# One layer's expert sum: rows of V gathered for one token block, float32 V products for the other

## The chip, the cores and the metric

The kernel runs on one core of a Trainium2 chip. The metric is the device time of one execution in microseconds (us). The engines are TensorE (PE; its weight loads are shown as PEld), VectorE (DVE), ScalarE (ACT), GpSimd (POOL) and SyncE (SP), which here only issues transfers. Sixteen DMA engines move the data of all queues.

## The reference

A network of two layers, followed by a second network, on 256 latent and 256 context tokens of 1024 channels. The part that matters is the expert layer (PEER) at the end of layer 1, on the 256 latent tokens:

```python
def peer_ffn(h, w_query, sub_keys, expert_u, expert_v):
    ...
    idx = jnp.take_along_axis(cand_i, pos, axis=-1).reshape(t_count, PEER_HEADS * PEER_TOPK)
    gate = jax.nn.softmax(top_s, axis=-1).reshape(t_count, PEER_HEADS * PEER_TOPK).astype(h.dtype)
    ...
    def block(args):
        tb, ib, gb = args
        act = jax.nn.gelu(jnp.einsum('pkd,pd->pk', expert_u[ib], tb), approximate=False) * gb
        return jnp.einsum('pk,pkd->pd', act, expert_v[ib])
```

`idx` holds the best 16 of 128 x 128 experts for each token and each of 8 heads; a `block` is 128 tokens. So each token has 128 chosen experts out of 16384. For each of them the token's vector is multiplied with a row of U (`peer_u`), passed through Gelu, weighted by its gate, and the rows of V (`peer_v`) are summed with these weights. U and V have 16384 rows of 1024 float32 numbers each, 64 MiB a table.

## The kernel before

The program is written with tiles and pools; the order of instructions on each engine and all waits come from a scheduler, which can move an instruction ahead of its place in the program when its inputs and buffers are free. Where the text calls `self.follow(d, mark[0])`, DVE instruction `d` is kept behind the one in `mark`. SP's queue, ScalarE's queue and GpSimd's queue each issue their transfers in order; an issue that waits for its buffer holds those behind it.

The function `peer1` does the expert layer of layer 1. Its 256 tokens are two blocks of 128, and each block takes another way.

- **The gathering block** (j=0) fetches, for each of its 128 slots (one slot is one chosen expert of every token), the 128 rows of U that its tokens chose, with an indirect DMA on GpSimd's queue (128 rows of 4 KB, 512 KB), into one of NR=6 buffers `rows`. One DVE instruction (L1281) multiplies them with the tokens `hn` and adds up along the row into a column of `dots`. `tick(n)` issues n such pairs from the list `todo`.
- **The dense block** (j=1) multiplies its tokens `hd` with all of U, in float32: `mm1` (L1253 to L1270) takes four row blocks of `peer_ut` (the transposed U) through four buffers `uf` (L1261, 512 KB each on SP's queue) and does 32 matmuls of 128 columns, then Gelu into `act`, [expert in block, block, token]. There are 32 calls.

The stages follow each other like this. First the queries, keys and the search for the best 16 (L1381 to L1394), with a `mm1` call and some gathers of U between. Then the one-hot stage of the dense block (L1461 to L1468), here called **B**: to put the gates in the layout of `act`, 32 steps of four tokens each build one-hot matrices, `oneR` (L1433) and three of four `oneL` (L1444) on DVE, the fourth on ScalarE, multiply them on PE (L1445) and copy them into `stage` (L1446); after every fourth step GpSimd multiplies `act` with the finished gates (L1466) or copies the gates in ahead of it (L1468). `between` runs after each step: it spreads the waiting U gathers over 27 steps and calls `mm1` after every third.

Then **C** (L1470 to L1480): Gelu on `dots`, times the gates, transposed, and a second one-hot stage of 32 steps for the gathering block, whose results go to a DRAM array `gd` (L1479); the remaining `mm1` calls stand between. At its end the pools of B and C are closed.

Then **D** (L1487 to L1499), the loop over 128 blocks of 128 rows of V, for both token blocks together: a block of V is loaded (`wf`, 512 KB on SP's queue) and split into a high and a low float32r part, 512 columns at a time, by ScalarE and DVE (`wsl`, `split`, L215 and L216); so are the activations (`gd` reloaded as `gt`, and `act`); and `mm3` (L249 to L251) does three float32r matmuls for each of two token blocks and two halves of the columns, twelve of 512 columns in all, into four PSUM accumulators. After the loop `_peer_out` transposes each sum and adds it into the residual `xT`.

The function `peer` of layer 0 is not touched, but is looked at: it also loads V blocks, loads `peer_ut` and gathers rows, of U and then of V, for one of its token blocks (L1154 to L1170), where the V rows are summed on DVE by L1169.

Of the kernel before, what the change touches and what calls it, by code (L numbers as in the profile page):

```python
# [170 lines left out]
class Net:  # L171
# [1031 lines left out]
    def peer1(self, xT, a, sh, gcol):  # L1203
# [3 lines left out]

# [6 lines left out]
        dr = pool("q_dr", bufs=1, space=DRAM)  # L1214
# [8 lines left out]
        def pf():  # L1223
            return fp.tile([128, 4, 128], F32, name="pf", bufs=6)
# [6 lines left out]
        hn = f0.tile([128, 8, 128], F32, name="hn")  # L1231
# [12 lines left out]
        gidx = f0.tile([128, 128], I32, name="gidx")  # L1244
        dots = f0.tile([128, 128], F32, name="dots")
# [28 lines left out]

        def tick(n):
            for _ in range(min(n, len(todo))):
                j = todo.pop(0)
                ug = f0.tile([128, 1024], F32, name="rows", bufs=NR)
                nc.gpsimd.indirect_dma_start(out=ug, out_offset=None, in_=A["peer_u1"],
                                             in_offset=bass.IndirectOffsetOnAxis(ap=gidx[:, j:j + 1], axis=0))  # L1280
                d = nc.vector.scalar_tensor_tensor(ug, ug, 1.0, hnf, op0=ALU.mult, op1=ALU.mult,  # L1281
                                                   accum_out=dots[:, j:j + 1])
                if mark[0] is not None:
                    self.follow(d, mark[0])
# [122 lines left out]
        gd = dr.tile([8, 128, 128, 16], F32, name="gd")  # L1407
        cols = []
        for j in (1, 0):
            ii = fs.tile([128, 128], I32, name="ii")  # L1410
            i2 = fl(idx[:, j])
            nc.vector.tensor_copy(ii, i2)
            nc.vector.tensor_single_scalar(ii, ii, 7, op=ALU.arith_shift_right)
            i1 = fs.tile([128, 128], F32, name="i1")
            nc.vector.tensor_copy(i1, ii)
            nc.vector.scalar_tensor_tensor(i2, i1, -128.0, i2, op0=ALU.mult, op1=ALU.add)
            p = pf()
            for c, t in enumerate((i1, i2, fl(gate[:, j]))):
                nc.tensor.transpose(p[:, c], t, self.ident)
            T = fs.tile([128, 5, 128], F32, name="igT", bufs=2)  # L1420
            nc.scalar.copy(T[:, 0], p[:, 0])
            nc.scalar.copy(T[:, 2:4], p[:, 1:3])
            mark[0] = nc.vector.tensor_scalar_mul(T[:, 1:5:3], T[:, 2:4], -1.0)
            cols.append(T)

        def onehot(T, t0, sg, engs, after):
# [28 lines left out]
        def between(q):  # L1455
            step[0] += 1
            tick(-(-len(todo) // max(1, 28 - step[0])))
            if step[0] % 3 == 0:
                mm1()

        for n in range(8):  # L1461
            sg = stage()
            onehot(cols[0], 16 * n, sg, "avvv", between)
            o, nb = 16 * n, 4 * done[0]
            gated[0] = o + 16
            nc.gpsimd.tensor_mul(act[:, 0:nb, o:o + 16], act[:, 0:nb, o:o + 16], sg[:, 0:nb])  # L1466
            if nb < 128:
                nc.gpsimd.tensor_copy(act[:, nb:128, o:o + 16], sg[:, nb:128])  # L1468

        T = cols[1]  # L1470
        nc.scalar.activation(dots, dots, AF.Gelu)
        nc.vector.tensor_mul(dots, dots, fl(gate[:, 0]))
        p = pf()
        nc.tensor.transpose(p[:, 0], dots, self.ident)
        nc.vector.tensor_copy(T[:, 3], p[:, 0])
        for g in range(8):
            sg = stage()
            onehot(T, g * 16, sg, "pvvv", lambda q: mm1() if q % 2 else None)
            nc.sync.dma_start(gd[g], sg)  # L1479
        assert done[0] == 32  # L1480
# [4 lines left out]
        acc = {(j, h): pacc.tile([128, 512], F32, name=f"acc{j}{h}") for j in range(2) for h in range(2)}  # L1485
        gt = None
        for b in range(128):  # L1487
            if b % 8 == 0:
                gt = ds_.tile([128, 8, 8, 16], F32, name="gt", bufs=2)
                nc.scalar.dma_start(gt, gd[:, :, b:b + 8, :].rearrange("g p i t -> p g i t"))  # L1490
            ah = ds_.tile([128, 256], F32R, name="ah", bufs=3)
            al = ds_.tile([128, 256], F32R, name="al", bufs=3)
            s3 = lambda t: t[:, 0:128].rearrange("p (g t) -> p g t", t=16)
            self.split(s3(ah), s3(al), gt[:, :, b % 8])
            self.split(ah[:, 128:], al[:, 128:], act[:, b])
            for h, w in enumerate(self.wsl(A["peer_v1"][b * 128:(b + 1) * 128], 512)):
                for j in range(2):
                    s = slice(j * 128, (j + 1) * 128)
                    self.mm3(acc[j, h], (ah[:, s], al[:, s]), w, b == 0, b == 127)  # L1499
        for j in range(2):  # L1500
            o = ds_.tile([128, 2, 512], F32, name="of", bufs=2)
            for h in range(2):
                nc.scalar.copy(o[:, h], acc[j, h])
            self._peer_out(2 + j, o, xT, gcol, pmm)
# [644 lines left out]
```

## Time and profile before

| | us |
|---|---|
| median of 3 runs | 3469.16 (3463.92 to 3498.61) |
| profiled execution | 3467.91 |
| its span, first to last instruction | 3466.1 |
| stage B, 2419.7 to 2537 | 117.3 |
| stage C, 2537 to 2626 | 89.0 |
| stage D, 2626 to 2978 | 352.0 |
| mean granted PE clock | 0.958 of full |

The stage borders are times from the span's start, read off the first and last instructions of the lines named above. The busy time of an engine is the union of its instructions, so that pipelined matmuls are not counted twice; a float32 matmul leaves two records. "DMA share" is the mean busy share of the 16 DMA engines (it can pass 1 a little), and GB/s what they moved.

### The profile page before, as it was taken

Reading aid. Unit: us, or ns where it says so; the run is one execution under the profiler, and the core shown is the slowest. Engines: PE = TensorE matmul, PEld = TensorE weight load, DVE = VectorE, ACT = ScalarE, POOL = GpSimd, SP = SyncE. Lnnn points to the kernel's source line nnn. Section 1 sums busy time; section 2 is a strip of 40 time slices with the busy share of each in tenths; the row PEclk is TensorE's granted clock in tenths of the full one; section 3 lists DMA queues with packets and bytes.
Section 4 is the critical chain, followed back from the end, with each engine's and each line's share of the span. In section 5 each row is a group of like instructions: output and inputs, shape, how many; then the busy total and the mean of one; then the engine's idle time right before and its main releaser. Section 6 shows DMA issues by size and latency. Waiting matters only on the chain. (4 is left out here: it accounts for less than half of the span.)

```text
span 3466.1 us, 54363 instructions
## 1 busy us (share of the span) xinstructions
PE 3164.8 (91%) x19470; PEld 2676.5 (77%) x19470; DVE 2438.0 (70%) x5726; ACT 1586.1 (46%) x3325; POOL 865.6 (25%) x781
## 2 busy tenths in 40 slices
PE   7989998898899999999999899965798999889899
PEld 4655657788889999999988658864787888777898
DVE  4664575688868777878877674787856666676666
ACT  3333334545963334433334463111535666653655
POOL 0010010466943333344432001444632000000000
PEclk9999999899999999999999999987899999899999
DMA  6355243233479898898877215998766777443465
GB/s 234 110 154 163 92 153 106 71 104 111 194 262 332 305 322 310 304 328 305 306 265 239 85 38 202 374 371 339 254 207 201 217 217 217 135 119 115 131 187 172
DMA packets 263855, 723.62 MB, mean 209 GB/s; under 512 B 22816, under 2 KB 97440, under 8 KB 259488
## 3 DMA queue, kind: packets, MB, share of 16 engines
q1 hardware_dynamic: 178496, 492.58, 42.6%
q0 software_dynamic: 55296, 201.35, 17.0%
q10 hardware_dynamic: 29792, 26.22, 2.3%
q8 instruction: 153, 2.51, 0.3%
q14 instruction: 118, 0.97, 0.1%
HBM read 681.00 MB, written 38.80 MB: 208 GB/s over the span
## 5 line engine op out<-in xcount | busy, mean ns | idle before, releaser
L215 ACT CAST wh<-wf 128x512 fp32r<-128x512 f32 (+1 forms) x906 | 560.3, 619 | 756.3 <-PE mm L250 288.3
L216 DVE TENSOR_TENSOR wl<-wf,wh 128x512 fp32r<-128x512 f32 (+1 forms) x820 | 563.7, 689 | 275.8 <-ACT wh L215 272.3
L251 PE MATMUL mm<-h_hi,wl 128*128 128x384 f32 x1024 | 347.2, 339 | 7.2 <-POOL wl L216 5.5
L249 PE MATMUL mm<-h_hi,wh 128*128 128x384 f32 x1024 | 348.8, 341 | 1.1 <-ACT wh L215 1.0
L250 PE MATMUL mm<-h_lo,wh 128*128 128x384 f32 x1024 | 346.0, 338 | 0.0
L251 PE MATMUL acc<-vh,al 128*128 128x512 f32 x768 | 300.7, 392 | 0.0
L250 PE MATMUL acc<-vl,ah 128*128 128x512 f32 x768 | 300.5, 391 | 0.0
L249 PE MATMUL acc<-vh,ah 128*128 128x512 f32 x768 | 298.7, 389 | 0.0
L1263 PE MATMUL mm<-hd,uf 128*128 128x128 f32 x2048 | 258.9, 285 | 28.8 <-DMA uf<-in_peer_ut_dram 24.5
L1263 PEld LDWEIGHTS mm<-hd,uf 128*128 128x128 f32 x2048 | 249.2, 201 | 34.1 <-DMA uf<-in_peer_ut_dram 14.8
L1157 POOL DMA_INDIRECT rows<-in_peer_v_dram,gidx x128 | 162.4, 1269 | 293.9 <-DVE hn L1169 273.5
L215 ACT CAST vh<-vf 128x512 fp32r<-128x512 f32 x256 | 158.8, 620 | 157.8 <-PE acc L251 151.4
L216 DVE TENSOR_TENSOR vl<-vf,vh 128x512 fp32r<-128x512 f32 x256 | 176.9, 691 | 67.0 <-ACT vh L215 65.1
L1157 POOL DMA_INDIRECT rows<-in_peer_u_dram,gidx x128 | 146.4, 1144 | 307.0 <-DVE rows L1163 297.9
L216 POOL TENSOR_TENSOR wl<-wf,wh 128x512 fp32r<-128x512 f32 x86 | 115.3, 1348 | 421.7 <-PE pa L581 251.5
L249 PE MATMUL acc<-wh,ah 128*128 128x512 f32 x512 | 200.6, 392 | 7.8 <-ACT ah L215 6.7
L1281 DVE SCALAR_TENSOR_TENSOR rows<-rows,hn 128x1024 f32<-128x1024 f32 x128 | 165.9, 1307 | 57.1 <-DMA rows<-in_peer_u_dram,gidx 56.8
L251 PEld LDWEIGHTS mm<-h_hi,wl 128*128 128x128 f32 x1024 | 193.5, 189 | 8.8 <-POOL wl L216 6.8
L251 PE MATMUL acc<-wh,al 128*128 128x512 f32 x512 | 200.2, 391 | 0.0
L250 PE MATMUL acc<-wl,ah 128*128 128x512 f32 x512 | 200.1, 391 | 0.0
L249 PEld LDWEIGHTS mm<-h_hi,wh 128*128 128x128 f32 x1024 | 193.9, 189 | 5.4 <-ACT wh L215 1.7
L250 PEld LDWEIGHTS mm<-h_lo,wh 128*128 128x128 f32 x1024 | 193.9, 189 | 3.7
(698 smaller groups left out, 7604.1 us busy)
## 6 DMA issues: line engine op xcount, KB each, us to landing
vf<-in_peer_v_dram SPq DMA_DIRECT2D x128, 512.0 KB, 5.9
wf<-in_peer_ut_dram SPq DMA_DIRECT2D x128, 512.0 KB, 6.3
uf<-in_peer_ut_dram SPq DMA_DIRECT2D x128, 512.0 KB, 6.7
wf<-in_peer_v_dram SPq DMA_DIRECT2D x128, 512.0 KB, 3.9
wa<-in_ada_w_dram SPq DMA_DIRECT2D x96, 512.0 KB, 4.3
gd<-stage SPq DMA_DIRECT2D x32, 1024.0 KB, 3.9
gt<-gd SPq DMA_DIRECT2D x48, 512.0 KB, 7.7
wf<-in_ffn_up_dram SPq DMA_DIRECT2D x44, 512.0 KB, 3.6
```

Of the source, the lines that this page charges most:

```text
L215: nc.scalar.copy(hi, src)
L216: return (eng or nc.vector).tensor_sub(lo, src, hi.bitcast(F32))
L249: nc.tensor.matmul(out, l[0], r[0], start=start, stop=False)
L250: nc.tensor.matmul(out, l[0], r[1], start=False, stop=False)
L251: nc.tensor.matmul(out, l[1], r[0], start=False, stop=stop)
L1157: nc.gpsimd.indirect_dma_start(out=t, out_offset=None, in_=A[src], in_offset=bass.IndirectOffsetOnAxis(ap=gidx[:, j:j + 1], axis=0))
L1263: nc.tensor.matmul(p[:, i], wf[:, k * 128:(k + 1) * 128], hd[:, k], start=(k == 0), stop=(k == 7))
L1281: d = nc.vector.scalar_tensor_tensor(ug, ug, 1.0, hnf, op0=ALU.mult, op1=ALU.mult, accum_out=dots[:, j:j + 1])
```

## The change

The gathering block now gathers rows of V as it gathered rows of U, and DVE adds them up; the one-hot stage C, `gd` and the gathering block's part of the loop over V go. The dense block's products with V become plain float32 matmuls without the split, two a block instead of twelve.

- `rows(src, j)` issues one gather of `peer_u1` or `peer_v1` into one of the six buffers, `tick_v(n)` issues n gathers of V from the list `left`, each with a DVE instruction that adds row times `dots` column to the accumulator `gf`. `rows`, `hn`, `gidx` and `dots` move to the pool that lives through the whole function; `gacc` takes the buffer of `hn`.
- `between` has done all U gathers after step 16, then weights `dots`, clears `gacc` on GpSimd, and does one V gather a step in the steps 17 to 32. `mm1` is called after every fourth step.
- The loop over V calls `mm1` in every fifth round until all 32 calls are out, loads a block of V into one of six buffers `vf`, does two float32 matmuls of 512 columns, and spreads the remaining 112 V gathers over its rounds.

```diff
         hf = fs.tile([128, 8, 256], F32, name="hf")
         self.norm_split(xT, [(256, 256, 0, a, sh)], None, None, lambda: pf().rearrange("p a b -> p (a b)"), t2, keep=hf)
-        hn = f0.tile([128, 8, 128], F32, name="hn")
+        hn = sb.tile([128, 8, 128], F32, name="hn")
...
         tv = f0.tile([128, nt, 8, 16], F32, name="tv")
         idx = f0.tile([128, nt, 8, 16], F32, name="idx")
         gate = f0.tile([128, nt, 8, 16], F32, name="gate")
-        gidx = f0.tile([128, 128], I32, name="gidx")
-        dots = f0.tile([128, 128], F32, name="dots")
+        gidx = sb.tile([128, 128], I32, name="gidx")
+        dots = sb.tile([128, 128], F32, name="dots")
...
         todo = []
+        def rows(src, j):
+
+            t = sb.tile([128, 1024], F32, name="rows", bufs=NR)
+            nc.gpsimd.indirect_dma_start(out=t, out_offset=None, in_=A[src],
+                                         in_offset=bass.IndirectOffsetOnAxis(ap=gidx[:, j:j + 1], axis=0))
+            return t
+
         def tick(n):
             for _ in range(min(n, len(todo))):
                 j = todo.pop(0)
-                ug = f0.tile([128, 1024], F32, name="rows", bufs=NR)
-                nc.gpsimd.indirect_dma_start(out=ug, out_offset=None, in_=A["peer_u1"],
-                                             in_offset=bass.IndirectOffsetOnAxis(ap=gidx[:, j:j + 1], axis=0))
+                ug = rows("peer_u1", j)
                 d = nc.vector.scalar_tensor_tensor(ug, ug, 1.0, hnf, op0=ALU.mult, op1=ALU.mult,
                                                    accum_out=dots[:, j:j + 1])
+                if mark[0] is not None:
+                    self.follow(d, mark[0])
+
+        left = list(range(128))
+
+        def tick_v(n):
+            for _ in range(min(n, len(left))):
+                j = left.pop(0)
+                d = nc.vector.scalar_tensor_tensor(gf, rows("peer_v1", j), dots[:, j:j + 1], gf,
+                                                   op0=ALU.mult, op1=ALU.add)
                 if mark[0] is not None:
                     self.follow(d, mark[0])
         nc.vector.tensor_mul(gate, gate, sm[:, :, :, None].to_broadcast(s4))
...
-        gd = dr.tile([8, 128, 128, 16], F32, name="gd")
-        cols = []
-        for j in (1, 0):
...
-        def onehot(T, t0, sg, engs, after):
+        ii = fs.tile([128, 128], I32, name="ii")
+        i2 = fl(idx[:, 1])
+        nc.vector.tensor_copy(ii, i2)
+        nc.vector.tensor_single_scalar(ii, ii, 7, op=ALU.arith_shift_right)
+        i1 = fs.tile([128, 128], F32, name="i1")
+        nc.vector.tensor_copy(i1, ii)
+        nc.vector.scalar_tensor_tensor(i2, i1, -128.0, i2, op0=ALU.mult, op1=ALU.add)
+        p = pf()
+        for c, t in enumerate((i1, i2, fl(gate[:, 1]))):
+            nc.tensor.transpose(p[:, c], t, self.ident)
+        T = fs.tile([128, 5, 128], F32, name="igT")
+        nc.scalar.copy(T[:, 0], p[:, 0])
+        nc.scalar.copy(T[:, 2:4], p[:, 1:3])
+        mark[0] = nc.vector.tensor_scalar_mul(T[:, 1:5:3], T[:, 2:4], -1.0)
+
+        def onehot(t0, sg, engs, after):
...
         step = [0]
         def between(q):
+            nonlocal gf, gacc
             step[0] += 1
-            tick(-(-len(todo) // max(1, 28 - step[0])))
-            if step[0] % 3 == 0:
+            if step[0] <= 16:
+                tick(-(-len(todo) // (17 - step[0])))
+            if step[0] == 16:
+                nc.scalar.activation(dots, dots, AF.Gelu)
+                nc.vector.tensor_mul(dots, dots, fl(gate[:, 0]))
+                gacc = sb.tile([128, 8, 128], F32, name="hn").rearrange("p (h a) b -> p h (a b)", h=2)
+                gf = gacc.rearrange("p h d -> p (h d)")
+                nc.gpsimd.memset(gacc, 0.0)
+            if step[0] > 16:
+                tick_v(1)
+            if step[0] % 4 == 0:
                 mm1()
+        gf = gacc = None
         for n in range(8):
             sg = stage()
-            onehot(cols[0], 16 * n, sg, "avvv", between)
+            onehot(16 * n, sg, "avvv", between)
             o, nb = 16 * n, 4 * done[0]
             gated[0] = o + 16
             nc.gpsimd.tensor_mul(act[:, 0:nb, o:o + 16], act[:, 0:nb, o:o + 16], sg[:, 0:nb])
             if nb < 128:
                 nc.gpsimd.tensor_copy(act[:, nb:128, o:o + 16], sg[:, nb:128])
-
-        T = cols[1]
-        nc.scalar.activation(dots, dots, AF.Gelu)
-        nc.vector.tensor_mul(dots, dots, fl(gate[:, 0]))
-        p = pf()
-        nc.tensor.transpose(p[:, 0], dots, self.ident)
-        nc.vector.tensor_copy(T[:, 3], p[:, 0])
-        for g in range(8):
-            sg = stage()
-            onehot(T, g * 16, sg, "pvvv", lambda q: mm1() if q % 2 else None)
-            nc.sync.dma_start(gd[g], sg)
-        assert done[0] == 32
         fr.close()
         ds_ = pool("q_ds", bufs=1)
         pacc = pool("q_acc", bufs=1, space=PSUM)
-        acc = {(j, h): pacc.tile([128, 512], F32, name=f"acc{j}{h}") for j in range(2) for h in range(2)}
-        gt = None
+        acc = [pacc.tile([128, 512], F32, name=f"acc{h}") for h in range(2)]
+        mark[0] = None
         for b in range(128):
-            if b % 8 == 0:
-                gt = ds_.tile([128, 8, 8, 16], F32, name="gt", bufs=2)
-                nc.scalar.dma_start(gt, gd[:, :, b:b + 8, :].rearrange("g p i t -> p g i t"))
-            ah = ds_.tile([128, 256], F32R, name="ah", bufs=3)
-            al = ds_.tile([128, 256], F32R, name="al", bufs=3)
-            s3 = lambda t: t[:, 0:128].rearrange("p (g t) -> p g t", t=16)
-            self.split(s3(ah), s3(al), gt[:, :, b % 8])
-            self.split(ah[:, 128:], al[:, 128:], act[:, b])
-            for h, w in enumerate(self.wsl(A["peer_v1"][b * 128:(b + 1) * 128], 512)):
-                for j in range(2):
-                    s = slice(j * 128, (j + 1) * 128)
-                    self.mm3(acc[j, h], (ah[:, s], al[:, s]), w, b == 0, b == 127)
-        for j in range(2):
-            o = ds_.tile([128, 2, 512], F32, name="of", bufs=2)
+            if b % 5 == 0:
+                mm1()
+            v = ds_.tile([128, 1024], F32, name="vf", bufs=6)
+            nc.sync.dma_start(v, A["peer_v1"][b * 128:(b + 1) * 128])
             for h in range(2):
-                nc.scalar.copy(o[:, h], acc[j, h])
-            self._peer_out(2 + j, o, xT, gcol, pmm)
+                nc.tensor.matmul(acc[h], act[:, b], v[:, h * 512:(h + 1) * 512], start=(b == 0), stop=(b == 127))
+            tick_v(-(-len(left) // max(1, 126 - b)))
+        assert done[0] == 32 and not left and not todo
+        o = ds_.tile([128, 2, 512], F32, name="of")
+        for h in range(2):
+            nc.scalar.copy(o[:, h], acc[h])
+        self._peer_out(3, o, xT, gcol, pmm)
+        self._peer_out(2, gacc, xT, gcol, pmm)
...
```

## Rows read from the trace of the kernel before

**Rows 1.** The page: span; busy time of each engine.

```profile
span 3466.1 us, 54363 instructions
...
PE 3164.8 (91%) x19470; PEld 2676.5 (77%) x19470; DVE 2438.0 (70%) x5726; ACT 1586.1 (46%) x3325; POOL 865.6 (25%) x781
```

**Rows 2.** Windows B, C, D: busy us (instructions) by engine, clock, DMA share, GB/s.

```profile
2419.70:2537.00 117.30, 89.02 (x618) 83.46 (x617) 106.70 (x213) 60.58 (x116) 67.40 (x45) 0.82 0.68 228
2537.00:2626.00 89.00, 80.45 (x672) 76.69 (x672) 47.05 (x129) 35.52 (x39) 42.52 (x32) 1.00 0.64 231
2626.00:2978.00 352.00, 347.94 (x1523) 287.87 (x1524) 237.28 (x509) 209.38 (x510) 0.00 (x0) 0.99 0.70 211
```

**Rows 3.** PE groups in B+C; `mm1` in C; one call.

```profile
L1263 PE MATMUL mm<-hd,uf 128*128 128x128 f32 x768 | 98.4, 283 | 0.9 <-ACT act L1270 0.6 <-DMA uf<-in_peer_ut_dram 0.4
L1445 PE MATMUL pf<-oneR,oneL 128*128 128x128 f32 x512 | 82.9, 306 | 32.2 <-DVE oneR L1433 12.1 <-DVE oneL L1444 9.3 <-POOL oneL L1444 7.3
...
2537.00:2626.00 89.00, 48.09 (x418) 47.31 (x418) 1.00 0.64 231
...
2562.90 7.31 PE L1263 MATMUL mm<-hd,uf 128*128 128x128 f32 x64
```

**Rows 4.** DVE's timeline, one step of B: start, duration, instruction.

```profile
2424.05 0.68 DVE L1433 TENSOR_TENSOR oneR<-io,igT 128x512 f32<-128x512 f32 x1
...
2425.43 1.21 DVE L1281 SCALAR_TENSOR_TENSOR rows<-rows,hn 128x1024 f32<-128x1024 f32 x1
...
2426.57 1.21 DVE L1281 SCALAR_TENSOR_TENSOR rows<-rows,hn 128x1024 f32<-128x1024 f32 x1
...
2427.72 0.68 DVE L1433 TENSOR_TENSOR oneR<-io,igT 128x512 f32<-128x512 f32 x1
```

**Rows 5.** U gathers and U products from B on.

```profile
L1279 POOL DMA_INDIRECT rows<-in_peer_u_dram,gidx x28: 933/1056/2132, 2419.5 to 2499.8; - x28
...
DMA to landing us min/median/max: 4.2/5.7/8.2
...
L1281 DVE SCALAR_TENSOR_TENSOR rows<-rows,hn 128x1024 f32<-128x1024 f32 x32 | 38.5, 1215 | 0.0
```

**Rows 6.** Layer 0: V product; last U product and the memset.

```profile
L1169 DVE SCALAR_TENSOR_TENSOR hn<-rows,dots,hn x128: 1277/1279/1287, 1460.5 to 1919.5; 128x1024 f32<-128x1024 f32 x128
...
1455.65 1.22 DVE L1163 SCALAR_TENSOR_TENSOR rows<-rows,hn 128x1024 f32<-128x1024 f32 x1
...
1456.94 0.95 POOL L1190 MEMSET hn<- 128x1024 f32 x1 [0.40 <-DVE rows L1163]
```

**Rows 7.** Float32 matmuls of 512 columns, elsewhere in the kernel.

```profile
2057.95 3.60 PE L1605 MATMUL psc<-kT,qz 128*128 128x512 f32 x8
...
L1605 PE MATMUL psc<-kT,qz x64: 590/592/697, 2018.6 to 2075.8; 128*128 128x512 f32 x64
```

**Rows 8.** Windows and DMA of 2340 to 2360.

```profile
2340.00:2360.00 20.00, 16.04 (x123) 14.96 (x122) 11.80 (x31) 2.09 (x6) 8.17 (x9) 0.95 1.03 418
...
q0 software_dynamic: 1164, 4.24, 51.9%
q1 hardware_dynamic: 1129, 4.10, 50.3%
...
uf<-in_peer_ut_dram SPq DMA_DIRECT2D x8, 512.0 KB, 8.4
rows<-in_peer_u_dram,gidx POOLq DMA_INDIRECT x8, 14.4
```

**Rows 9.** Window in layer 0.

```profile
1250.00:1750.00 500.00, 500.00 (x2529) 455.11 (x2528) 397.10 (x580) 198.55 (x362) 190.65 (x155) 1.00 0.90 311
```

**Rows 10.** Two windows ahead of B; SP's queue in the first.

```profile
2300.00:2320.00 20.00, 5.19 (x22) 4.24 (x21) 19.71 (x47) 1.78 (x5) 12.00 (x10) 0.70 0.95 349
2370.00:2420.00 50.00, 18.34 (x127) 17.18 (x126) 35.55 (x85) 5.09 (x14) 28.06 (x25) 0.66 0.79 293
...
q1 hardware_dynamic: 505, 1.88, 25.5%
```

More of the change, by code (lines that the diff above doesn't have):

```diff
@@ L1213, in peer1 @@
         pmm = pool("q_mm", bufs=1, space=PSUM)
-        dr = pool("q_dr", bufs=1, space=DRAM)
         hd = sb.tile([128, 8, 128], F32, name="hd")
@@ L1406, in peer1 @@
         fl = lambda t: t.rearrange("p a b -> p (a b)")
-        gd = dr.tile([8, 128, 128, 16], F32, name="gd")
-        cols = []
-        for j in (1, 0):
[L1410 to L1416, printed above, removed]
-            p = pf()
[L1418 to L1424, printed above, removed]
-        def onehot(T, t0, sg, engs, after):
+        ii = fs.tile([128, 128], I32, name="ii")
[13 more added lines that the diff above has]
+        def onehot(t0, sg, engs, after):
             for q in range(4):
@@ L1468, in peer1 @@
                 nc.gpsimd.tensor_copy(act[:, nb:128, o:o + 16], sg[:, nb:128])
-        T = cols[1]
-        nc.scalar.activation(dots, dots, AF.Gelu)
-        nc.vector.tensor_mul(dots, dots, fl(gate[:, 0]))
-        p = pf()
-        nc.tensor.transpose(p[:, 0], dots, self.ident)
-        nc.vector.tensor_copy(T[:, 3], p[:, 0])
-        for g in range(8):
-            sg = stage()
-            onehot(T, g * 16, sg, "pvvv", lambda q: mm1() if q % 2 else None)
-            nc.sync.dma_start(gd[g], sg)
-        assert done[0] == 32
         fr.close()
```

## Prediction

> **What bounds the kernel now.** I read the page's header and its table of engines first [rows 1]: TensorE (PE) is busy 91% of a 3466.1 us span, but that is an average over stages. The change touches only `peer1`, so the next view is the table of windows over the part of `peer1` that it rewrites [rows 2]. Three stages follow each other there: B, the one-hot stage of the dense token block (117.3 us); C, the one-hot stage of the gathering block (89.0 us); D, the loop over 128 row blocks of V (352.0 us); 558.3 us together. The reader should see that each has another limit. In B VectorE (DVE) is busy 106.7 of 117.3 us. In C PE is busy 80.5 of 89. In D PE is busy 347.9 of 352 at nearly full clock, 352/128 = 2.75 us for the twelve matmuls of a block, while DMA moves only 211 GB/s. Before B, the queries already stream `peer_ut` and gather rows of U side by side; the change leaves that alone, and it is the nearest picture of what D turns into.
>
> **Stage C goes.** The second `onehot` loop, the transposes for j=0, the eight stores of `gd` and their reload fall away: 89.0 us. Not all of it is saved: of the twelve first products (`mm1`) still open at the start of B (768 records, 64 to a call), 418 records, 6.5 calls, ran in C [rows 3]. They move into B or D and are counted there, each with its four loads on SP's queue, its Gelu on ScalarE and its multiplication on DVE.
>
> **Stage B gets longer.** DVE sets B: PE's waits for its one-hots end on DVE first of all [rows 3]. One step there is one `oneR` and three `oneL`; in the timeline two gather products and one such step take 2427.72-2424.05 = 3.67 us, of it 1.145 us for each product and 1.38 us for the rest [rows 4]. The 32 U products left at the start of B [rows 5] come two a step in 16 steps instead of two and later one, which changes nothing in sum. New are 16 V products, one a step in the second half. None runs here before, but layer 0 has the same instruction at 1.279 us [rows 6]: 16 x 1.28 = 20.5 us, all on the bounding engine. At the change from U to V the accumulator takes the buffer of `hn`: GpSimd's memset waits for the last U product, the first V product for the memset and its gather, and the next one-hots stand behind that product on DVE. Layer 0 makes the same turn: the memset starts at 1456.94, 0.07 us after the end of the last U product, and takes 0.95 us [rows 6]. The turn costs between nothing and 8 us (a gather of 1.06 us to issue and 5.7 to land in B [rows 5], behind the memset); I take 2, nearest to layer 0's turn. Gelu on `dots` waits on ScalarE for the same product, with copies of `stage` behind it, inside that time. GpSimd has room: 67.4 us busy of 117.3, plus 16 gathers of 1.1 us. One `mm1` in four steps instead of three gains nothing, since PE isn't what B waits for. B: 117.3+20.5+2 = 140 us, with bounds of 127 (the new work first fills DVE's 10.6 us of idle time) and 146.
>
> **Stage D, TensorE.** Per block, twelve float32r matmuls become two float32 matmuls of 512 columns. A float32 matmul leaves two records; eight records of that shape in a row take 3.60 us, the last of them 0.59, so starts are (3.60-0.59)/7 = 0.43 us apart [rows 7]. A matmul is 0.86 us, a block 1.72 instead of 2.75, 128 blocks 220 us. Weight loads are in that figure. The splits on ScalarE and DVE vanish, but PE hardly waited for them; they save nothing. Nine `mm1` calls are written into the loop, but calls move ahead of their place: 20 of 32 were done when B began, though the program had put out 15. I count five of the twelve in D, bounds 3 and 9. A call is 7.3 us [rows 3], so PE has 220+37 = 257 us of work. PE no longer sets the loop.
>
> **Stage D, transfers.** Now 112 gathers of V rows run beside 128 V loads and 20 `uf` loads, 524288 bytes each: 260 x 0.524 = 136.3 MB. The row that prices this is the stretch from 2340 to 2360, where `uf` loads and U gathers run together and little else does [rows 8]: 418 GB/s with the engines full, 51.9% on the gather queue and 50.3% on SP's, eight of each issued in 20 us, so one of each per 2.5 us. Bytes alone give 136.3/0.418 = 326 us. But the two streams don't end together: 112 gathers at 2.51 us last 281 us; SP's queue has by then moved 112 of its 148 loads, and the other 36 go at PE's 1.72 us, 62 us. Together 343 us, with bounds of 326 (the streams end together) and 371 (nine calls in D: 281+52 x 1.72). DVE has 112 x 1.28 = 143 us here and GpSimd 112 x 1.06 = 119 [rows 5]: both are covered, and would show only if the transfers took less. Behind a V product that waits for its gather stand the multiplications of `mm1`; five calls, each late by a gather at most, with two `ga` buffers between them and PE, cost nothing. SP's queue holds V and `uf` loads in order, with six and four buffers; a load that waits for its buffer holds those behind it, as it does in [rows 8]. The first `vf` buffers lie over `io` and `stage`, free when the last one-hots are; B counts to the last gate product on GpSimd, which is later. I take 3 us for the handover, bounds 0 and 10.
>
> **The sum.** B, handover and D after: 140+3+343 = 486 us in place of 558.3, a saving of 72. The profiled execution took 3467.9 us (1.8 outside its span), 1.3 below the median of the three runs, so its scale is kept: 3467.9-72 = 3396 us. The lower bounds, 127+0+326 = 453, give 3363; the upper, 146+10+371 = 527, give 3437. What follows `peer1` is unchanged: two output blocks as before, the gathered one already in place.
>
> **A rule that speaks against it.** The stretch in [rows 8] shows 418 GB/s into this core from two queues. The Trainium skill, page "DMA: Bandwidth & Descriptors", section Specifications, gives about 358 GB/s as what HBM yields to one core; by that D's bytes take an estimated 381 us and the time is 3434. The trace doesn't agree: 418 GB/s stood for 20 us.
>
> **The rivals.**
> (1) The transfers hold less, and the kernel gets slower. In layer 0, where the same mix of V loads, loads of `peer_ut` and gathers runs, the mean is 311 GB/s [rows 9]. At that rate D takes 136.3/0.311 = 438 us and the time is 3491; at 290 GB/s it is 3523. It turns slower below 136.3/(558.3-143) = 0.328, 328 GB/s. For it: thousands of scattered 4 KB rows over 300 us, not 20. Against: PE was busy 500 of 500 us in that window, so 311 was what it asked for.
> (2) The same place at a middle rate: the stretch from 2300 to 2320 had 349 GB/s at a DMA share of 0.95 [rows 10]. D takes 391 us, the time is 3443. The page's rule above would act like this. Against: SP's queue carried only 25.5% there, so it was short of work.
> (3) PE's clock. PE has 257/343 = 75% of D to work, and two stretches in which it waited have a granted clock of 0.70 and 0.66 [rows 10], a mix of 1.2 and 2.4 GHz. At 0.66 PE needs 389 us and the time is 3442; it decides below 0.75. Against: at 1.2 GHz a block takes 3.4 us, more than its load, so PE would wait no more, and where it works without a pause the clock is 0.99, in D [rows 2]; in the stretch that resembles D it is 0.95 [rows 8].
> (4) The change doesn't overlap: gathers run behind the products instead of beside them. D is 257+112 x 1.3 = 403 us, the time 3456. Against: a gather needs nothing in the loop but one of six buffers.
>
> **Chances.** The forecast 0.76, (1) 0.08, (2) 0.06, (3) 0.06, (4) 0.04. A measurement here tells about 1% (35 us) from no change; the three runs spread over 3464 to 3499. The forecast's own range, 3363 to 3437, lies nearly all below 3433; its tip, (2), (3), (4) and part of (1) count as the same, the rest of (1) as slower: 0.75, 0.19 and 0.06. The range takes in (2) and (3), 3363 to 3444.
>
> **What the profile after would show.** B near 140 us with DVE over 90% busy and a short stall at its middle; no stores of `gd`; D near 345 us, DMA at 400 GB/s or more for its first 280 us with half on the gather queue, PE waiting for `vf` and its V records 0.43 us apart, then a last stretch without gathers in which PE is full. The prediction is wrong if the rate stays under 350 GB/s while both queues have work, if PE is always busy at a clock under 0.75, if gathers still run when the products have ended, or if B passes 150 us because GpSimd's gate products and gathers hold each other up.

## The result and the profile after

The changed kernel takes 3382.3 us in the median of four runs (3376.3 to 3392.6), the kernel before 3471.4 us beside it: a ratio of 0.973, 95% interval 0.967 to 0.979. The forecast was 3396 us, its range 3363 to 3444. The profiled execution took 3384.5 us with a span of 3382.4, 83.7 us less than the span before.

The first view is the same as in [rows 2], busy time by engine in windows, for the new stages: B, the part of D in which rows of V are gathered, and the rest of D.

```profile
2421.50:2552.70 131.20, 96.06 (x662) 90.98 (x662) 126.03 (x218) 60.32 (x111) 103.64 (x66) 0.78 0.83 294
2552.70:2827.50 274.80, 220.25 (x715) 105.13 (x714) 146.53 (x120) 4.18 (x7) 103.75 (x108) 0.98 1.02 416
2827.50:2897.60 70.10, 70.10 (x165) 30.89 (x164) 1.28 (x1) 0.58 (x1) 0.00 (x0) 1.00 0.80 288
```

Read each row for the engine with no room left. In the first it is DVE (126 of 131 us), as before. In the second no engine is full (PE is busy 220 of 275 us), but the DMA share is 1.02 at 416 GB/s. In the third PE is busy for all of it at full clock. The DMA view of the second window gives the two queues:

```profile
DMA packets 31398, 114.42 MB, mean 416 GB/s; under 512 B 3488, under 2 KB 3488, under 8 KB 31388
...
q1 hardware_dynamic: 15911, 57.97, 51.8%
q0 software_dynamic: 15477, 56.33, 50.2%
```

The gather queue (q0) and SP's queue (q1) have half each, at the rate of [rows 8], for 275 us instead of 20. PE's timeline shows what that makes of a block of V, before and after the last gather:

```profile
2566.24 1.98 PE L1501 MATMUL acc<-vf,act 128*128 128x512 f32 x4 [0.47 <-DMA vf<-in_peer_v_dram]
2568.78 1.98 PE L1501 MATMUL acc<-vf,act 128*128 128x512 f32 x4 [0.55 <-DMA vf<-in_peer_v_dram]
2571.24 1.99 PE L1501 MATMUL acc<-vf,act 128*128 128x512 f32 x4 [0.48 <-DMA vf<-in_peer_v_dram]
...
2826.92 70.65 PE L1501 MATMUL acc<-vf,act 128*128 128x512 f32 x164 [0.46 <-DMA vf<-in_peer_v_dram]
```

A block is four records (two float32 matmuls). The starts are 2.46 to 2.54 us apart, and each ends a wait for the load of `vf`. From 2826.9 on, 164 records run without a wait, 0.43 us each, 1.72 us a block.

For the comparison of runs, the stages are cut at the same instructions in every kernel: B from the first `oneR` on DVE to the end of the last copy into `act` on GpSimd, D from there until the last V product is done. On PE that is the start of the copy that reads the finished accumulator, on DVE the end of the product; the later one counts. The columns are us; "calls" are `mm1` records divided by 64. Each run's rows below come from its own profiled execution; the medians are of four runs each, and each ratio is to runs of the kernel before that were made beside it. "e1" and so on are the experiments of the next section.

```
kernel    median  ratio to before [95%]     B      D     B+D  calls in B, D
before    3471.4                          117.4  440.7  558.0  5.5  6.5   (D: stages C and D)
after     3382.3  0.973 [0.967, 0.979]    131.4  343.8  475.2  6.4  5.7
e10       3383.0  0.976 [0.973, 0.979]    130.9  345.2  476.0  6.3  5.7   (after, once more)
e1        3298.4  0.950 [0.945, 0.954]    131.5  264.0  395.5  6.3  5.7
e2        3357.1  0.967 [0.962, 0.971]    131.4  326.4  457.8  6.5  5.6
e3        3393.5  0.976 [0.972, 0.981]    112.0  371.8  483.9  4.0  8.0
e4        3371.9  0.972 [0.967, 0.977]    122.7  343.4  466.1  6.2  5.8
e5        3569.7  1.029 [1.026, 1.032]    118.3  535.9  654.2  5.5  6.5   (D: stages C and D)
e6        3375.1  0.975 [0.971, 0.979]    137.5  332.5  470.0  7.8  4.2
e7        3349.5  0.966 [0.964, 0.968]    122.6  327.9  450.5  6.2  5.8
e8        3354.3  0.969 [0.964, 0.974]    127.3  319.4  446.7  8.4  3.7
e9        3396.1  0.981 [0.979, 0.983]    132.0  363.6  495.6  6.5  5.6
```

The change saves 82.9 us inside the rewritten stages (558.04-475.16); all else adds up to 0.8 us of the span. The same kernel again (e10) gives the same stages within 1.4 us, while its profiled time was 3393.3, 8.8 us longer: its first `mm1` call of layer 1 starts 12.5 us later (2145.5 against 2133.0), at a mean clock of 0.92 in the first 600 us against 0.95. So a few microseconds are read below from the stages, not from the totals.

### The profile page after: what moved, and what is told of

Same layout as the page of the kernel before. It is cut to its first block, busy times and chain, and to the rows that moved or that the text cites. A ratio compares the mean times of both kernels' runs of the same rounds, so it can differ in the third digit from the quotient of the medians.

```text
span 3382.4 us, 50442 instructions
## 1 busy us (share of the span) xinstructions
PE 3035.1 (90%) x18186; PEld 2460.9 (73%) x18186; DVE 2318.0 (69%) x5208; ACT 1343.3 (40%) x2775; POOL 962.7 (28%) x878
## 5 line engine op out<-in xcount | busy, mean ns | idle before, releaser
L215 ACT CAST wh<-wf 128x512 fp32r<-128x512 f32 (+1 forms) x650 | 401.8, 620 | 672.7 <-PE mm L250 279.5
L216 DVE TENSOR_TENSOR wl<-wf,wh 128x512 fp32r<-128x512 f32 (+1 forms) x564 | 386.2, 687 | 175.1 <-ACT wh L215 171.3
L1261 PE MATMUL mm<-hd,uf 128*128 128x128 f32 x2048 | 271.9, 294 | 44.1 <-DMA uf<-in_peer_ut_dram 43.0
L1261 PEld LDWEIGHTS mm<-hd,uf 128*128 128x128 f32 x2048 | 260.4, 208 | 56.0 <-DMA uf<-in_peer_ut_dram 32.0
L1501 PE MATMUL acc<-vf,act 128*128 128x512 f32 x512 | 242.5, 611 | 41.4 <-DMA vf<-in_peer_v_dram 41.4
L1294 DVE SCALAR_TENSOR_TENSOR hn<-rows,dots,hn 128x1024 f32<-128x1024 f32 x128 | 164.2, 1283 | 127.9 <-DMA rows<-in_peer_v_dram,gidx 127.9
L1501 PEld LDWEIGHTS acc<-vf,act 128*128 128x128 f32 x512 | 91.3, 190 | 187.9 <-DMA vf<-in_peer_v_dram 100.2
L251 PEld LDWEIGHTS mm<-h_hi,wl 128*128 128x128 f32 x1024 | 194.5, 190 | 10.1 <-POOL wl L216 6.8
```

The source lines that it names most:

```text
L215: nc.scalar.copy(hi, src)
L216: return (eng or nc.vector).tensor_sub(lo, src, hi.bitcast(F32))
L251: nc.tensor.matmul(out, l[1], r[0], start=False, stop=stop)
L1261: nc.tensor.matmul(p[:, i], wf[:, k * 128:(k + 1) * 128], hd[:, k], start=(k == 0), stop=(k == 7))
L1294: d = nc.vector.scalar_tensor_tensor(gf, rows("peer_v1", j), dots[:, j:j + 1], gf, op0=ALU.mult, op1=ALU.add)
L1501: nc.tensor.matmul(acc[h], act[:, b], v[:, h * 512:(h + 1) * 512], start=(b == 0), stop=(b == 127))
```

## The experiments

Each run takes away, moves or adds one thing. e5 starts from the kernel before, all others from the changed kernel; e7 and e8 put edits together and e10 has none. The quoted text under each edit is what was expected of it.

**e1: what D costs without its gathers.** The 112 gathers of V rows that the program has in D, and their products, are left out.

```
-            tick_v(-(-len(left) // max(1, 126 - b)))
-        assert done[0] == 32 and not left and not todo
+        assert done[0] == 32 and not todo
```

> Leaves out the 112 gathers of V rows in stage D and the DVE instructions that add them up, so that the gathering block's sum holds only the first 16 slots; everything else stays. Theory (in D the sixteen DMA engines are the bound while gathers and loads share them, PE has slack): without gathers the loads run ahead of PE, D falls from 344.7 us to PE's own work, 128 x 1.72 us for the V products plus about 5 to 6 calls of mm1 at 7.3 us, 257 to 265 us with the handover; the time falls by 80 to 88 us, to about 3300. Rival (D is set by PE at a lowered clock, or by its single waits for loads whatever else moves): D stays above 320 us and the time above 3360.

The window of D in this kernel:

```profile
2542.40:2806.40 264.00, 261.59 (x876) 138.32 (x875) 6.15 (x9) 4.18 (x8) 0.01 (x1) 0.99 0.84 296
```

PE is now the full engine, 261.6 of 264.0 us at 0.99. The forecast put its work at 257 us with five `mm1` calls in D; with the 5.7 that ran there it would have been 262. The gathers cost 343.8-264.0 = 79.8 us on top of it, 0.7 us for each gather of 128 rows, though none of them uses PE: they take transfer time from the V loads.

**e2: a second queue for the loads.** If the queues share evenly, two queues of loads beside one of gathers should get more than half. Every other V load is issued by ScalarE.

```
-            nc.sync.dma_start(v, A["peer_v1"][b * 128:(b + 1) * 128])
+            (nc.scalar if b % 2 else nc.sync).dma_start(v, A["peer_v1"][b * 128:(b + 1) * 128])
```

> The loads of V blocks in D go to SP's and ScalarE's queue in turn, nothing else changes. Theory (the DMA engines share themselves out by queue, one turn for each queue that has work, which is why gathers held half and ended 70 us before the loads): with three queues the loads get up to two thirds, a V block takes about 1.9 us instead of 2.5 while gathers run, and the two streams end nearly together; D falls from 344.7 to 326 to 332 us, the time by 12 to 18. Rival A (the share goes by bytes in flight, or by kind of transfer): the V blocks stay 2.5 us apart, D stays within 4 us. Rival B (a second issuing engine costs): D grows, as ScalarE's Gelu for mm1 waits behind loads that wait for their buffers.

DMA in the middle of its D, 2700 to 2857:

```profile
DMA packets 18089, 65.90 MB, mean 420 GB/s; under 512 B 2011, under 2 KB 2011, under 8 KB 18085
...
q0 software_dynamic: 6853, 24.95, 38.9%
q10 hardware_dynamic: 5904, 21.50, 33.5%
q1 hardware_dynamic: 5328, 19.40, 30.2%
```

The rate is the same (420 GB/s); the gather queue falls from half to 39% and the loads rise to 64%, 78 loads in 157 us or one in 2.0 us. So the share goes largely by queue, though not in exact thirds. The products on PE end 315.2 us after B, the V products on DVE 326.4, and D is 17.4 us shorter. That is near the bound of 326 us which the forecast gave for streams that end together, and it shows that the last stretch of the changed kernel, in which PE runs alone, comes from how the queues share, not from the bytes.

**e3: no V products in B.** All 128 gathers of V move into D.

```
-            if step[0] > 16:
-                tick_v(1)
```

> All 128 V gathers and products are placed in D, none in B. Theory (DVE sets B, so each of the 16 V products there is paid in full): B falls by 16 x 1.28 = 20 us, from 131 to about 111; D has 16 gathers more, each 2.5 us of shared transfers in place of a block at 1.72 in the unshared end, so it grows by 16 x (2.51-1.72) = 12 us; together 8 us less, time about 3375. Rival (V products in B fit into time in which DVE would wait anyway): B stays within 5 us, D grows by 12, the time rises to about 3394.

B becomes 19.3 us shorter, near the 20 expected, but not by 16 products alone: the scheduler still moves three V products ahead of B's end (17 ran there in the changed kernel), DVE's busy time falls by 15.4 us and its idle time by 4.0. D becomes 28.0 us longer, more than twice the 12 expected. The reason is in the windows of the `mm1` matmuls alone (PE busy, PEld busy), B and the gathering part of D:

```profile
2429.00:2540.20 111.20, 36.77 (x248) 34.05 (x249) 0.76 0.66 231
2540.20:2855.10 314.90, 66.79 (x523) 61.84 (x521) 0.98 1.02 416
```

Since the edit takes no call out of B, the expectation had left the calls where they were; that is where it failed. 248 records ran in B, 4.0 calls, against 6.4 in the changed kernel, and 31 `uf` loads were issued after B instead of 21. With 14 V products more, D's growth is an estimated 14 x 79.8/111 = 10.1 us (e1's price, 111 products) and 10 x 1.72 = 17.2 us (the block's pace), together 27.3 of the 28.0. The V products in B are worth their place by 8.7 us of B+D.

**e4: the gate products on DVE.** In the changed kernel GpSimd multiplies `act` by the staged gates in B. DVE does it here.

```
-            nc.gpsimd.tensor_mul(act[:, 0:nb, o:o + 16], act[:, 0:nb, o:o + 16], sg[:, 0:nb])
+            mark[0] = nc.vector.tensor_mul(act[:, 0:nb, o:o + 16], act[:, 0:nb, o:o + 16], sg[:, 0:nb])
```

> The eight multiplications of act with the finished gates in B go from GpSimd to DVE; the copies beside them stay on GpSimd. Theory (while GpSimd multiplies two SBUF operands, DVE's one-hot instructions stand still: one of them takes 3.9 to 5.0 us instead of 0.34, which happened six to eight times in B, some 25 us together): on DVE a multiplication takes 1.1 to 1.7 us, 11 us together, the long one-hots are gone, B falls by 12 to 16 us, the time to about 3370. Rival (the long one-hots only take up time in which DVE would have waited for something else, and 11 us of new DVE work is added): B grows by up to 11 us, the time to 3384 to 3395.

DVE's groups in B, first of the changed kernel, then of this one (group | busy us, mean ns | idle before):

```profile
L1453 DVE TENSOR_SCALAR oneL<-io,igT 128x128 f32<-128x128 f32 x96 | 45.1, 524 | 0.0
L1284 DVE SCALAR_TENSOR_TENSOR rows<-rows,hn 128x1024 f32<-128x1024 f32 x32 | 40.8, 1306 | 1.5 <-DMA rows<-in_peer_u_dram,gidx 1.4
L1442 DVE TENSOR_TENSOR oneR<-io,igT 128x512 f32<-128x512 f32 x32 | 22.7, 709 | 1.1 <-issue 1.1
L1294 DVE SCALAR_TENSOR_TENSOR hn<-rows,dots,hn 128x1024 f32<-128x1024 f32 x17 | 21.7, 1276 | 0.0
L1266 DVE TENSOR_TENSOR act<-act,ga 128x64 f32<-128x64 f32 (+6 forms) x7 | 5.3, 759 | 0.0
```

```profile
L1453 DVE TENSOR_SCALAR oneL<-io,igT 128x128 f32<-128x128 f32 x96 | 29.6, 366 | 0.0
...
L1486 DVE TENSOR_TENSOR act<-act,stage 128x1024 f32<-128x1024 f32 (+7 forms) x8 | 11.7, 1466 | 2.2 <-ACT stage L1455 2.0
```

DVE takes on eight instructions, 11.7 us, and is still done earlier: its 96 one-hots drop by 15.5 us and its U products by 2.8, and one V product fewer falls into B. B is 8.7 us shorter, less than the 12 to 16 expected, and D is the same. So the same one-hot is slower while GpSimd multiplies. The expectation had overrated how much: in the changed kernel's B five one-hots take 2.4 to 4.4 us instead of 0.34 and one U product 4.0 instead of 1.2, some 17 us too long together, and not 25. The last section shows one case.

**e5: float32 products without the gathering.** The kernel before, stage C included, with the products of both token blocks in D as plain float32 matmuls.

```
-            self.split(s3(ah), s3(al), gt[:, :, b % 8])
-            self.split(ah[:, 128:], al[:, 128:], act[:, b])
...
-                    self.mm3(acc[j, h], (ah[:, s], al[:, s]), w, b == 0, b == 127)
+            gb = ds_.tile([128, 128], F32, name="gb", bufs=3)
+            nc.vector.tensor_copy(gb.rearrange("p (g t) -> p g t", t=16), gt[:, :, b % 8])
+            v = ds_.tile([128, 1024], F32, name="vf", bufs=6)
+            nc.sync.dma_start(v, A["peer_v1"][b * 128:(b + 1) * 128])
+            for h in range(2):
+                for j, s in enumerate((gb, act[:, b])):
+                    nc.tensor.matmul(acc[j, h], s, v[:, h * 512:(h + 1) * 512], start=(b == 0), stop=(b == 127))
```

> The kernel before with one half of the change alone: in D its products with V are float32 matmuls on the unsplit block (four of 512 columns a block, two token blocks by two halves), the gathering block still goes through the one-hot stage C and gd, and nothing is gathered from V. Theory (the gain is that half of D's products and all of C go to transfers that had room; float32 by itself is dearer on PE than three float32r matmuls): a block takes 4 x 0.86 = 3.44 us on PE instead of 2.75, D 440 us instead of 352, the time about 3558. Rival (the splits on ScalarE and DVE were what held D, so that unsplit products are faster by themselves): D at or below 352 us, the time at or below 3470.

PE's timeline in its D:

```profile
2700.45 1.02 PE L1497 MATMUL acc<-vf,act 128*128 128x512 f32 x2
2701.30 1.02 PE L1497 MATMUL acc<-vf,gb 128*128 128x512 f32 x2
2702.16 1.02 PE L1497 MATMUL acc<-vf,act 128*128 128x512 f32 x2
```

A float32 matmul starts 0.86 us after the one before it, as worked out from [rows 7]. Four a block are 3.43 us against 2.75 before, and the kernel is 2.9% slower; C and D together take 95.2 us more, where 88 were expected. Float32 by itself is the dearer form here. In the change it pays; the next run shows that side.

**e9: the change without float32.** The dense block's products are split into float32r again, three matmuls for each.

```
+            ah = ds_.tile([128, 128], F32R, name="ah", bufs=3)
+            al = ds_.tile([128, 128], F32R, name="al", bufs=3)
+            self.split(ah, al, act[:, b])
             for h in range(2):
-                nc.tensor.matmul(acc[h], act[:, b], v[:, h * 512:(h + 1) * 512], start=(b == 0), stop=(b == 127))
+                wh = self.wp.tile([128, 512], F32R, name="wh", bufs=3)
+                wl = self.wp.tile([128, 512], F32R, name="wl", bufs=3)
+                self.split(wh, wl, v[:, h * 512:(h + 1) * 512])
+                self.mm3(acc[h], (ah, al), (wh, wl), b == 0, b == 127)
```

> The changed kernel with the other half of the change undone: the dense block's products with V stay as they were before, three float32r matmuls for each half of the columns on blocks that ScalarE and DVE split (six matmuls of 0.226 us a block, 1.35 us on PE instead of 1.72; 1.67 us of splits on DVE a block, besides the V product of 1.28). V blocks come through the same six buffers. Theory (D is set by transfers at half a share each, and DVE stands right behind them: 1.67 + 1.28 = 2.95 us a round against 2.5 for the shared transfers, with splits queued behind V products that wait for their gathers): D is 112 x 2.95 + 16 x 1.67 = 357 us against 344, the time 10 to 20 longer, about 3395. Rival (PE's time decides, and 1.35 us a block is better than 1.72): D falls by up to 26 us, at the end where nothing is shared, the time to 3356 to 3375.

D is 19.8 us longer than in the changed kernel, where 13 were expected. In the middle of D, DVE's timeline has a round of 2.60 us a block, full without a gap:

```profile
2702.73 1.27 DVE L1294 SCALAR_TENSOR_TENSOR hn<-rows,dots,hn 128x1024 f32<-128x1024 f32 x1
2703.93 0.28 DVE L216 TENSOR_TENSOR al<-act,ah 128x128 fp32r<-128x128 f32 x1
2704.13 1.28 DVE L216 TENSOR_TENSOR wl<-vf,wh 128x512 fp32r<-128x512 f32 x2
2705.33 1.27 DVE L1294 SCALAR_TENSOR_TENSOR hn<-rows,dots,hn 128x1024 f32<-128x1024 f32 x1
```

Of the round, 1.2 us go to the V product and the rest to the splits; 2.95 us were expected. Up to the last V product on DVE, 336.8 us after B instead of 275.8, DVE is busy 298.4 us and waits 21.9 for ScalarE's half of the split and 13.8 for gathers, and the transfers move 383 GB/s at a DMA share of 0.98. So the splits fill DVE and delay the V products; how much of the delay comes from the lower transfer rate was not tried. The two halves of the change can be priced: gathering alone saves 62.4 us (558.04-495.61), float32 on top of it 20.4 us.

**e6: one `mm1` in three steps of B.** As in the kernel before; the forecast held that the fourth step gains nothing over the third.

```
-            if step[0] % 4 == 0:
+            if step[0] % 3 == 0:
```

> The changed kernel with mm1 called after every third step of B instead of every fourth, so that two more calls stand in B's part of the program. Theory (B is set by DVE and leaves PE and DMA room, D pays 1.72 us for each load on SP's queue at its unshared end): about two calls more run in B, D loses 8 loads, 14 us, B stays within 3 us, the time falls to about 3368. Rival (the scheduler has already pulled as many calls into B as buffers and PSUM allow): the calls stay where they are and the time within 5 us of 3382.

It moves 1.5 calls from D to B. D is 11.2 us shorter where 14 were expected, B 6.1 us longer where 3 were allowed, B+D 5.2 us shorter. DVE's row for the multiplication behind `mm1` tells where most of B's growth comes from:

```profile
L1266 DVE TENSOR_TENSOR act<-act,ga 128x128 f32<-128x128 f32 (+6 forms) x9 | 6.3, 698 | 4.6 <-POOL act L1488 4.6
```

DVE again waits 4.6 us for GpSimd's copies into `act`. In the total the gain isn't told apart from none (0.975 against 0.973).

**e7 and e8: together.** e7 is e2 and e4 in one kernel, e8 is e7 with e6's line as well.

```
+            mark[0] = nc.vector.tensor_mul(act[:, 0:nb, o:o + 16], act[:, 0:nb, o:o + 16], sg[:, 0:nb])
...
+            (nc.scalar if b % 2 else nc.sync).dma_start(v, A["peer_v1"][b * 128:(b + 1) * 128])
```

> The changed kernel with both edits that gained alone: V loads on SP's and ScalarE's queue in turn, and the gate products of B on DVE. Theory (they act on different stages with different bounds, queue shares in D and DVE in B): the gains add, B about 121 us, D with the last gathers about 327, the time 25 + 10 below 3382, about 3347. Rival (what B is shortened by comes back in D, as transfers that B had carried have to be moved there at the full engines): B 121 but D longer by about as much, the time stays near 3357.

> The same as the kernel with both edits, and mm1 after every third step of B. Theory (D is now set by the sum of its bytes at about 419 GB/s, and B has transfer room): two calls, 4.2 MB, move from D to B and D falls by about 10 us, the time to about 3337. Rival (calls stay where they are, or PE becomes B's bound): no change within 5 us.

The two gains nearly add up: 17.4 us (e2) and 8.7 us (e4) by themselves, 24.7 together. With 3349.5 us e7 is the fastest version; its interval (0.964 to 0.968) lies below that of the changed kernel in e10 (0.973 to 0.979). e8 shortens B+D by 3.8 us more, and its total isn't told apart from e7's. D falls by 8.5 us, near the 10 expected, but B grows by 4.7: DVE's gate products wait 5.7 us for ScalarE's copy into `stage` instead of 2.2. PE's timeline at the end of e8's D shows what now ends it:

```profile
2860.87 0.64 PE L1519 MATMUL mm<-ident,of 128*128 128x128 f32 x4
2861.71 0.66 PE L1519 MATMUL mm<-ident,of 128*128 128x128 f32 x4 [0.20 <-issue]
2899.68 2.15 PE L1519 MATMUL mm<-ident,hn 128*128 128x128 f32 x8 [37.31 <-DVE xT L1522]
```

The dense block is done, and PE stands 37 us until the gathered block's accumulator (`hn`) is complete: the gathers are now what ends last.

**e10** is the changed kernel once more, beside e9.

> The changed kernel once more, as the measure for small differences. Any theory: time within 10 us of 3382, B 131 and D 344 within 2 us; how far the time ahead of B moves between executions shows how much of a difference in total time is not from the edits.

## Why the prediction was right, and where it was off

**D, transfers: the mechanism right, the sum closer than its parts.** One gather and one load in 2.51 us was right: block starts are 2.46 to 2.54 us apart. e2 shows that the queues' sharing makes the lone last stretch, and e1 that D takes only 264 us without its gathers. The forecast had 281 us with gathers and 62 us after them, 343. From the first V product on PE, 272.2 us passed until the last one on DVE, and 68.0 us more on PE: 340.2. The first part is shorter since more gathers were issued in B than the 16 written there, as GpSimd's row of that stage shows:

```profile
L1276 POOL DMA_INDIRECT rows<-in_peer_v_dram,gidx x21 | 33.9, 1613 | 8.3 <-DVE hn L1294 3.7 <-DVE oneL L1453 3.2 <-issue 1.4
```

That left 107, not 112; at 2.51 us they are 269 us. The loads then had less of the shared time, and 41 blocks (164 records) instead of 36 loads were left for the last stretch. That the two misses nearly cancel is luck in part: the forecast did not see that gathers run ahead of their place.

The rates of rivals (1) and (2), 311 and 349 GB/s, did not come: 416 GB/s stood. The 358 GB/s per core that the Trainium skill, page "DMA: Bandwidth & Descriptors", section Specifications, gives does not hold for this stretch. The Trainium skill, same page, section Bandwidth, tells of 425 GB/s for a 16 MB transfer while the pair's other core is idle; the 416 to 420 GB/s here, from a kernel that runs on one core, are near that.

**D, clock and overlap: right.** The granted clock was 0.98 while PE waited 0.5 us in each block (rival 3 put 0.66), and gathers and products ran side by side (rival 4).

**D, `mm1` and handover: near.** Five calls with 20 loads were counted. By PE's records 5.7 ran in D; their loads run ahead, and 21 were issued after B. V products on PE began at 2556.65, 3.6 us after B, where 3 were allowed.

**B: the term that was mis-sized.** 140 us were forecast, 131.4 came. The sum had 20.5 us for V products and 2 us for the turn, 22.5 on top of 117.3. DVE's busy time did rise by 126.0-106.7 = 19.3 us, but its idle time fell from 10.6 to 5.2 us. The forecast's lower bound had new work fill that idle time; its sum took none of it. In the kernel before, 8.8 us of it are one wait, DVE's groups in B there having this row:

```profile
L1268 DVE TENSOR_TENSOR act<-act,ga 128x128 f32<-128x128 f32 (+6 forms) x9 | 3.7, 411 | 8.8 <-POOL act L1468 8.8
```

In the changed kernel the same instruction (L1266, under e4) has no idle time before it. With `mm1` in every fourth step it no longer comes just when GpSimd copies into `act`; e6 puts the third step back and half of the wait returns (4.6 us). So "gains nothing" was wrong: the step looked at what B waits for on PE, and the cost was on DVE, which bounds the stage. What decides how often the two meet, beyond that one line, was not tried. GpSimd was underrated too, with no cost here: 67.4 us and 16 gathers of 1.1 make 85, and it was busy 103.6, mostly since 21 gathers of V took 1.61 us each to issue.

**The turn from U to V** was put at 2 us, and no wait for it shows on DVE. GpSimd had issued four V gathers before it cleared the accumulator (start, duration):

```profile
2487.38 0.94 POOL L1276 DMA_INDIRECT rows<-in_peer_v_dram,gidx  x1 [0.30 <-DVE oneL L1453]
...
2494.22 0.95 POOL L1474 MEMSET hn<- 128x1024 f32 x1 [1.15 <-DVE rows L1284]
```

DVE meanwhile made one-hots, and its first V product began without an idle gap before it:

```profile
2490.15 4.00 DVE L1284 SCALAR_TENSOR_TENSOR rows<-rows,hn 128x1024 f32<-128x1024 f32 x1 [1.38 <-DMA rows<-in_peer_u_dram,gidx]
...
2495.93 1.27 DVE L1294 SCALAR_TENSOR_TENSOR hn<-rows,dots,hn 128x1024 f32<-128x1024 f32 x1
```

The last U product did wait 1.38 us for its gather and took 4.00 us instead of 1.21, but it did so beside a gate product that GpSimd ran from 2489.45 to 2492.26; the last section comes to that.

**The sum.** B came out 8.6 us shorter than forecast, the loop of D 2.8 (340.2 against 343), the handover 0.6 longer, and everything outside 0.6 shorter: 11.4 us. The forecast less the profiled execution, 3396-3384.5, is 11.5; the rest is rounding.

## What to carry to other kernels

Where two queues feed one loop, sum the bytes for the lower bound, but time each queue's own list at its share: the one with the longer list runs on alone at the pace of whatever then limits it, and moving some of it to a third queue can recover the difference (17 us here). Before work is moved into or out of a stage, follow what is scheduled by progress rather than by place; calls of `mm1` drifted by two or three between stages and were worth nearly as much as the edit (17.2 beside 19.3 us in e3). On a stage that one engine bounds, list that engine's own idle time by releaser first: new work fills it, or a new spacing removes it.

## What was not expected of the hardware

**GpSimd's arithmetic slows DVE's one-hots.** In the changed kernel, DVE and GpSimd side by side:

```profile
2519.56 4.96 DVE L1453 TENSOR_SCALAR oneL<-io,igT 128x128 f32<-128x128 f32 x3
2524.44 1.27 DVE L1294 SCALAR_TENSOR_TENSOR hn<-rows,dots,hn 128x1024 f32<-128x1024 f32 x1
```

```profile
2517.79 2.66 POOL L1276 DMA_INDIRECT rows<-in_peer_v_dram,gidx  x1 [0.30 <-DVE oneL L1453]
2520.46 3.00 POOL L1486 TENSOR_TENSOR act<-act,stage 128x1344 f32<-128x1344 f32 x1
2523.39 0.78 POOL L1488 COPY act<-stage 128x704 f32<-128x704 f32 x1
```

Three one-hots, 0.85 to 0.94 us in undisturbed steps, take 4.96 us while GpSimd multiplies and copies; e4 removes the multiplication and their mean falls from 524 to 366 ns. The kernel before has the same: five of its one-hots take 2.4 to 3.6 us beside GpSimd's products, so it is not new with the change. The Trainium skill, page "GPSIMD Engine Reference", section Key points, says that GpSimd shares its interfaces to the on-chip memory with VectorE, with contention with VectorE's instructions that run in a two-port performance mode or have two inputs there. The U product of 4.00 us above has two; the one-hots read one tensor and two columns of scalars, and no row here shows in which mode they ran.

**The start of the kernel moves from run to run.** Before layer 1's first `mm1` the second profiled execution of the changed kernel (e10) is 12.5 us behind the first, and e8's is 36 us behind it, with mean clocks of 0.95, 0.92 and 0.89 in the first 600 us. The stretch from 500 to 600 us has a granted clock of 0.92 in the first, 0.76 in e10 and 0.74 in e8. What sets that clock was not tried.
